# Low parts of the plain weight pages: from a VectorE subtraction to an accumulating DMA

## The chip, the cores and the metric

The kernel runs on one core of a Trainium2 chip. The core has five engines with an instruction stream each: TensorE (PE, its weight loads shown apart as PEld), VectorE (DVE), ScalarE (ACT), GpSimd (POOL) and SyncE (SP), and 16 DMA engines that serve all DMA queues. The metric is device time in microseconds (us) of one execution; lower is better.

## The reference, cut to what matters

Two layers of a decoder trunk in float32 on x of [512, 1024]. Each layer has three residual sub-layers, each ended by a layer norm: a token mixer (one wide input projection, sliding-window attention over 16 heads, a gated linear recurrence, three more 1024x1024 products), cross-attention into 256 memory tokens, and a SwiGLU block.

```python
for l in range(DEPTH):                        # DEPTH = 2
    mix = hybrid_mixer(h, w_in[l], ..., w_br_rnn[l], w_br_attn[l], sinks[l], w_out[l], cos, sin)
    h = layer_norm(DEEPNORM_ALPHA * h + mix, ln1_g[l], ln1_b[l])
    h = layer_norm(DEEPNORM_ALPHA * h + cross_attention(h, mem, cq_w[l], ckv_w[l], co_w[l]), ...)
    h = layer_norm(DEEPNORM_ALPHA * h + swiglu(h, ffn_wi[l], ffn_wo[l]), ln3_g[l], ln3_b[l])
```

All matrix products go through weights that are read once per execution from device memory.

## The kernel before, in words

**Products in three terms.** A float32 operand is held as two float32r parts, hi (the value rounded) and lo (value minus hi). A product A @ B is summed on PE from three float32r products: hi*hi, hi*lo and lo*hi (`mtile`, L259; `step` in `out_norm`, L442; the memory-value loop in `cross`, L913). The weight's hi part is used in two products of three and its lo part in the third, so of the first three matmuls of a page the third is the first to need lo.

**Weight pages.** `Weights` (L45) streams the weights as pages of [128, 1024] float32 (512 KB) in the order in which they are used; `schedule_weights` (L614) lists them, 128 plain pages per layer and 40 more that take another way (`split_quad`, the first product of the SwiGLU block, which the change does not touch). A page's life, in `split` (L94): SyncE has loaded it into one of four `raw` buffers (`dma`, L84); ACT writes the rounded copy `whi` (L110); DVE writes `wlo` = raw - whi (L111); then loads are issued until four pages past this one are under way (L113). The parts take two of the 32 pages of the pool `pg`. A raw buffer is free for the next load when both readers are done, and the SyncE queue waits for that at the load's issue; everything that SyncE issues later waits behind it.

**How far ahead.** `next` (L193) hands out page i after it has put the split of pages up to i + 2 (`la` = 2) into the instruction streams; so the split of page i + 2 stands, in the order of each engine, before the evictions of page i's product. Where a stage ends, `ensure` (L189) puts in several splits at once: the five last row pages of an output projection (L463) and some of the next stage (L466). Instructions of one engine run in the order that the framework fixed when the kernel was built, which is mostly the order of the program.

**Stages of a layer**, with their pages and PE work per page: keys, values and two query blocks (4 pages); six query and twelve gate blocks beside the attention units (18 pages, a page is 24 matmuls of 512 columns); the attention branch (8); the recurrent input with its convolution, four elementwise instructions per block on ACT and DVE (8, "conv stage" below); the recurrence's gates (4); four gate blocks with the recurrence's exponentials on ACT (4) and the GeLU gate with the scan (8), together "recurrence stage"; the recurrent branch (8); the output projection by rows (8, of which 5 are held for the end); cross-attention keys (8, 24 matmuls of only 256 columns, "key stage"); queries (8); memory values (8, 12 matmuls of 512 columns, "value stage"); the cross output projection by rows (8); the SwiGLU block's first four pages and, after the 40 others, its 22 row pages.

**GpSimd before.** It subtracts in `split_quad` (L139, 40 times), copies a sink column for each attention unit (L560, 64 times), and adds the last bias (L419). It issues no DMA.

Of the kernel before, what the change touches and what calls it, by code (L numbers as in the profile page):

```python
# [9 lines left out]
AF = mybir.ActivationFunctionType  # L10
ALU = mybir.AluOpType
AX = mybir.AxisListType
PSUM = bass.MemoryType.PSUM
# [27 lines left out]
def f(ap):  # L41
    return ap.bitcast(F32)


class Weights:  # L45
    """Streams the weights in the order in which they are used: each page of
    [128, 1024] is loaded once and split exactly into two float32r parts."""

    def __init__(self, K):
        self.K = K  # L50
# [43 lines left out]
    def split(self):  # L94
        j = self.n_split
        if j >= len(self.specs):
            return
        while self.n_dma <= j:
            self.dma()
        if j in self.quad:  # L100
            self.drain()
            self.gen = self.split_quad(j)
            self.drain()
            return
        self.n_split += 1
        nc = self.K.nc
        raw = self.raw.pop(j)
        hi = self.K.page(F32R, "whi")
        lo = self.K.page(F32R, "wlo")
        nc.scalar.activation(out=hi, in_=raw, func=AF.Copy)  # L110
        nc.vector.tensor_sub(out=lo, in0=raw, in1=f(hi))  # L111
        self.parts[j] = (hi, lo)
        while self.n_dma < min(len(self.specs), j + 1 + N_RAW):  # L113
            self.dma()

    def split_quad(self, j):
        """Operands of the seven products that replace the eight block products
        of two column blocks (rows halved, columns the two blocks)."""
        while self.n_dma <= j + 1:
            self.dma()  # L120
        self.n_split += 2
        K, nc = self.K, self.K.nc
        a, b = self.raw.pop(j), self.raw.pop(j + 1)
        a1, a2, b1, b2 = a[:, :S], a[:, S:], b[:, :S], b[:, S:]

        def one(x):
            t = K.page(F32R, "wq")
            K.split_to(t[:, :S], t[:, S:], x)
            return t[:, :S], t[:, S:]

        def pair():
            hi, lo = K.page(F32R, "wqh"), K.page(F32R, "wql")
            return [(hi[:, :S], lo[:, :S]), (hi[:, S:], lo[:, S:])]

        tt = nc.vector.tensor_tensor
        o = self.parts[j] = {}
        s12, s34 = K.page(F32, "s12"), K.page(F32, "s34")
        s1, s2, s4, s3 = s12[:, :S], s12[:, S:], s34[:, :S], s34[:, S:]
        nc.gpsimd.tensor_tensor(out=s3, in0=a1, in1=b1, op=ALU.subtract)  # L139
        tt(out=s1, in0=b1, in1=b2, op=ALU.add)  # L140
        yield
        o["A11"] = one(a1)
        yield
        tt(out=s2, in0=s1, in1=a1, op=ALU.subtract)
        o["S1"], o["S2"] = pair()
        yield
        K.split_to(*o["S1"], s1)
        yield
        tt(out=s4, in0=a2, in1=s2, op=ALU.subtract)
        yield  # L150
        K.split_to(*o["S2"], s2)
        yield
        o["A12"] = one(a2)
        yield
        o["S4"], o["S3"] = pair()
        K.split_to(*o["S4"], s4)
        yield
        K.split_to(*o["S3"], s3)
        yield
        o["A22"] = one(b2)  # L160
        while self.n_dma < min(len(self.specs), j + 2 + N_RAW):
            self.dma()
# [38 lines left out]
class Trunk:  # L201
# [66 lines left out]
    def xs(self, c0=0, c1=S):  # L268
        return lambda k: (self.xT[:, k, 0, c0:c1], self.xT[:, k, 1, c0:c1])
# [20 lines left out]
                           self.xs(hf * 256, hf * 256 + 256))  # L290
        return out

    # ---- layer norm over token tiles, and the transposed operand for what follows
    def to_xT(self, t):
        for q in range(2):
            ps = self.ps("pt")
            for i in range(4):
                c = (q * 4 + i) * P
                self.tp(ps[:, i * P:(i + 1) * P], self.xt[t][:, c:c + P])
            v = ps.rearrange("p (k s) -> p k s", k=4)  # L300
            self.split_to(self.xT[:, q * 4:q * 4 + 4, 0, t * P:(t + 1) * P],
                          self.xT[:, q * 4:q * 4 + 4, 1, t * P:(t + 1) * P], v)
            if self.want_T:
                self.x_parts(t, q, v)
        self.x_done[t] = True

    def x_parts(self, t, q, v):
        """The sums of x's blocks that the seven products take, split in two parts."""
        nc = self.nc
        tt = nc.vector.tensor_tensor  # L310
        if t < 2:
            if q == 0:
                self.Bf[t] = self.page(F32, "Bf").rearrange("p (k s) -> p k s", k=ND)
            nc.scalar.activation(out=self.Bf[t][:, q * 4:q * 4 + 4, :], in_=v, func=AF.Copy)
            return
        b = self.Bf[t - 2]
        h = lambda name: self.half(name=name).rearrange("p (k s) -> p k s", k=4)
        if q == 0:
            self.t1, self.b12 = h("t1"), h("b12")
            tt(out=self.t1, in0=v, in1=b[:, 0:4, :], op=ALU.subtract)  # L320
            nc.scalar.activation(out=self.b12, in_=v, func=AF.Copy)
            if t == 2:
                self.T = {n: [self.page(F32R, n + p).rearrange("p (k s) -> p k s", k=4) for p in "hl"]
                          for n in ("T1", "T2", "T3", "T4")}
            return
        t2, t3, t4 = h("t2"), h("t3"), h("t4")
        tt(out=t2, in0=v, in1=self.t1, op=ALU.subtract)
        tt(out=t3, in0=v, in1=self.b12, op=ALU.subtract)
        tt(out=t4, in0=b[:, 4:8, :], in1=t2, op=ALU.subtract)
        c = slice((t - 2) * P, (t - 1) * P)  # L330
        for n, x in (("T1", self.t1), ("T2", t2), ("T3", t3), ("T4", t4)):
            self.split_to(self.T[n][0][:, :, c], self.T[n][1][:, :, c], x)
        self.Bf[t - 2] = None
# [9 lines left out]
            self.tick()  # L343

    def proj_pair(self):
        """Two column blocks of x @ W; returns the first as an SBUF tile, the second
        as its halves over the tokens (one in PSUM, one in SBUF)."""
        nc = self.nc
        o = self.W.next_quad()
        b1, b2, b3 = (self.ps(n)[:, :256] for n in ("q1", "q2", "q3"))  # L350
        T = {n: (lambda k, n=n: (self.T[n][0][:, k, :], self.T[n][1][:, k, :])) for n in self.T}
        xs = lambda k0, c0: (lambda k: (self.xT[:, k0 + k, 0, c0:c0 + 256], self.xT[:, k0 + k, 1, c0:c0 + 256]))
        c1, c3 = (lambda t: (t[:, :256], t[:, 256:]))(self.half(name="c13"))
        c2, c5 = (lambda t: (t[:, :256], t[:, 256:]))(self.half(name="c25"))
        g = self.half(name="gt")
        cp = lambda out, in_: nc.scalar.activation(out=out, in_=in_, func=AF.Copy)  # L356
        add = lambda out, x, y: nc.vector.tensor_tensor(out=out, in0=x, in1=y, op=ALU.add)
        self.quad_product(b1, o["A11"], xs(0, 0), True)
        cp(c1, b1)
        self.W.piece()  # L360
        self.quad_product(b2, o["S1"], T["T1"], True)
        cp(c5, b2)
        self.W.piece()
        self.quad_product(b1, o["S2"], T["T2"], False)
        cp(c2, b1)
        self.W.piece()
        self.quad_product(b2, o["S4"], xs(4, 256), False)
        add(g[:, 256:], c2, b2)
        self.W.piece()
        self.quad_product(b1, o["S3"], T["T3"], False)  # L370
        cp(c3, b1)
        self.W.piece()
        self.quad_product(b3, o["A12"], xs(4, 0), True)
        add(g[:, :256], c1, b3)
        self.W.piece()
        self.quad_product(b1, o["A22"], T["T4"], False)
        add(c3, c3, c5)
        self.W.piece()
        return g, b1, c3
# [48 lines left out]

    def out_norm(self, act, nk, res, alpha, eps, gv, bv, last=False, prefetch=0, between=None,
                 want_T=False, restore=False):  # L430
        """x_tok <- LN(alpha * x_tok + act @ W), W streamed by rows."""
        nc = self.nc
        g = self.page(F32, "ln_g")
        nc.sync.dma_start(out=g, in_=gv.partition_broadcast(P))
# [41 lines left out]
            if between:  # L476
                between(t)

    # ---- sliding-window attention
    def rope(self, ps, eng=None):  # L480
        nc = self.nc
        sh = self.half(name="sh")
        nc.vector.stream_shuffle(sh, ps, ROPE_SWAP)
        q = self.half(name="qr")
        nc.vector.tensor_tensor(out=q, in0=ps, in1=self.ropeC, op=ALU.mult)
        eng = eng or (nc.vector if ROPE_V else nc.gpsimd)
        eng.tensor_tensor(out=sh, in0=sh, in1=self.ropeS, op=ALU.mult)
        eng.tensor_tensor(out=q, in0=q, in1=sh, op=ALU.add)
        return q
# [120 lines left out]
                                        in0=av[0:64, :, e, :], in1=t[0:64, :, e, :], op=ALU.add)  # L610
            self.split_to(ya[:, 0, cs], ya[:, 1, cs], y)

    # ---- one layer
    def schedule_weights(self):  # L614
        a, W = self.a, self.W
        for l in range(self.L):
# [453 lines left out]
```

## Time and profile before

| | us |
|---|---|
| runs shown: median of 2 (lowest, highest) | 1901.68 (1901.50, 1901.86) |
| span of the profiled execution, first to last instruction | 1899.8 |
| PE busy in it | 1881.5 (99%) |
| DVE busy | 1327.2 (70%) |
| ACT busy | 928.9 (49%) |
| POOL busy | 112.3 (6%) |
| DMA packets' share of the 16 engines' span | 37% |

The span leaves out what lies before the first and after the last instruction; the runs shown are 1.9 us longer than it. Busy time of PE contains what a pipelined matmul waits behind the one before. A row of the timeline gives the start in us from the span's start, the duration in us, engine, line, operation, the tile written and the tiles read, their shapes and types, how many instructions are merged, and in brackets the idle time of the engine just before with what ended it.

### The profile page before, as it was taken

Reading aid. Unit: us, or ns where it says so; the run is one execution under the profiler, and the core shown is the slowest. Engines: PE = TensorE matmul, PEld = TensorE weight load, DVE = VectorE, ACT = ScalarE, POOL = GpSimd, SP = SyncE. Lnnn points to the kernel's source line nnn. Section 1 sums busy time; section 2 is a strip of 40 time slices with the busy share of each in tenths; the row PEclk is TensorE's granted clock in tenths of the full one; section 3 lists DMA queues with packets and bytes.
Section 4 is the critical chain, followed back from the end, with each engine's and each line's share of the span. In section 5 each row is a group of like instructions: output and inputs, shape, how many; then the busy total and the mean of one; then the engine's idle time right before and its main releaser. Section 6 shows DMA issues by size and latency. Waiting matters only on the chain.

```text
span 1899.8 us, 27941 instructions
## 1 busy us (share of the span) xinstructions
PE 1881.5 (99%) x10874; PEld 1654.2 (87%) x10874; DVE 1327.2 (70%) x2267; ACT 928.9 (49%) x1760; POOL 112.3 (6%) x114
## 2 busy tenths in 40 slices
PE   8999999999999999999999999999999999999998
PEld 7888888889888999998898888888898889999886
DVE  5997367567557988873579963675665589888634
ACT  4676168333443665652246751773244536565521
POOL 0000000000000122100000000000000001221001
PEclk9999999999999999999999999999999999999999
DMA  6433233354244233354213441333542513333531
GB/s 171 112 101 107 60 100 89 100 177 145 67 149 129 79 112 101 109 190 139 72 45 101 110 124 45 100 89 100 177 123 78 182 63 112 100 110 102 188 100 45
DMA packets 275445, 209.19 MB, mean 110 GB/s; under 512 B 7536, under 2 KB 253808, under 8 KB 275312
## 3 DMA queue, kind: packets, MB, share of 16 engines
q1 hardware_dynamic: 275312, 207.40, 36.7%
q8 instruction: 85, 1.39, 0.3%
q14 instruction: 48, 0.39, 0.1%
HBM read 192.69 MB, written 8.39 MB: 106 GB/s over the span
## 4 chain that ended last, share of the span: by engine, by line
PE 96%; DVE 3%; DMA 1%; SPq 0%; ACT 0%; issue 0%; DVEq 0%
PE ps L232 45%; PE acc L232 21%; PE q L232 21%; PE cv L232 2%; PE sc L232 2%; PE av L232 1%; PE cs L232 1%; PE pT L236 1%; PE pt L236 1%; DMA raw<-in_w_in_dram 1%; DVE xT L253 0%; PE cT L236 0%; DVE y L405 0%; DVE st L398 0%; DVE y L396 0%; DVE nw L408 0%
## 5 line engine op out<-in xcount | busy, mean ns | idle before, releaser
L232 PE MATMUL ps<-xT,whi 128*128 128x512 f32 (+1 forms) x1984 | 563.2, 370 | 3.4 <-ACT whi L110 2.3
L111 DVE TENSOR_TENSOR wlo<-raw,whi 128x1024 fp32r<-128x1024 f32 x256 | 310.6, 1222 | 142.0 <-ACT whi L110 113.9
L232 PEld LDWEIGHTS ps<-xT,whi 128*128 128x128 f32 x1984 | 345.5, 189 | 58.7 <-ACT whi L110 2.7
L232 PE MATMUL ps<-xT,wlo 128*128 128x512 f32 (+1 forms) x992 | 363.2, 367 | 0.8 <-DVE wlo L111 0.8
L110 ACT ACTIVATE whi<-raw 128x1024 fp32r<-128x1024 f32 x256 | 266.5, 1053 | 126.9 <-PE acc L232 52.4
L232 PE MATMUL acc<-whi,hs 128*128 128x512 f32 x704 | 217.9, 390 | 0.5 <-ACT hs L252 0.5
L232 PEld LDWEIGHTS ps<-xT,wlo 128*128 128x128 f32 x992 | 187.2, 189 | 34.1 <-DVE wlo L111 1.0
L232 PEld LDWEIGHTS acc<-whi,hs 128*128 128x128 f32 x704 | 132.1, 188 | 28.3 <-ACT hs L252 0.9
L139 POOL TENSOR_TENSOR s<-raw 128x512 f32<-128x512 f32 x40 | 82.9, 2074 | 1209.6 <-DVE y L405 878.4
L232 PE MATMUL acc<-wlo,hs 128*128 128x512 f32 x352 | 137.0, 389 | 0.0
L232 PE MATMUL q<-xT,wq 128*128 128x256 f32 x960 | 126.7, 281 | 0.0
L232 PEld LDWEIGHTS q<-xT,wq 128*128 128x128 f32 x960 | 119.4, 189 | 0.0
L253 DVE TENSOR_TENSOR wql<-s,wqh 128x512 fp32r<-128x512 f32 x160 | 116.7, 757 | 0.0
L252 ACT ACTIVATE wqh<-s 128x512 fp32r<-128x512 f32 x160 | 96.1, 624 | 18.9 <-DVE s L140 9.2
L356 ACT ACTIVATE c<-q 128x256 f32<-128x256 f32 x160 | 60.7, 379 | 84.5 <-PE q L232 83.1
L253 DVE TENSOR_TENSOR wq<-raw,wq 128x512 fp32r<-128x512 f32 x120 | 82.8, 690 | 0.0
L232 PE MATMUL acc<-whi,mg 128*128 128x512 f32 x256 | 80.2, 391 | 0.0
L232 PE MATMUL acc<-whi,cO 128*128 128x512 f32 x256 | 80.2, 391 | 0.0
L232 PE MATMUL ps<-ya,whi 128*128 128x512 f32 x256 | 78.9, 389 | 0.0
L232 PE MATMUL ps<-yr,whi 128*128 128x512 f32 x256 | 78.8, 389 | 0.0
L232 PEld LDWEIGHTS acc<-wlo,hs 128*128 128x128 f32 x352 | 66.1, 188 | 13.5
L252 ACT ACTIVATE wq<-raw 128x512 fp32r<-128x512 f32 x120 | 74.5, 621 | 0.0
(218 smaller groups left out, 3718.9 us busy)
## 6 DMA issues: line engine op xcount, KB each, us to landing
raw<-in_ffn_wi_dram SPq DMA_DIRECT2D x88, 512.0 KB, 3.9
raw<-in_w_in_dram SPq DMA_DIRECT2D x84, 512.0 KB, 3.9
raw<-in_ffn_wo_dram SPq DMA_DIRECT2D x44, 512.0 KB, 3.7
raw<-in_ckv_w_dram SPq DMA_DIRECT2D x32, 512.0 KB, 4.3
raw<-in_w_br_attn_dram SPq DMA_DIRECT2D x16, 512.0 KB, 3.8
raw<-in_w_br_rnn_dram SPq DMA_DIRECT2D x16, 512.0 KB, 4.0
raw<-in_w_out_dram SPq DMA_DIRECT2D x16, 512.0 KB, 3.6
raw<-in_cq_w_dram SPq DMA_DIRECT2D x16, 512.0 KB, 5.0
```

The costliest lines, as they stand in the source:

```text
L110: nc.scalar.activation(out=hi, in_=raw, func=AF.Copy)
L111: nc.vector.tensor_sub(out=lo, in0=raw, in1=f(hi))
L139: nc.gpsimd.tensor_tensor(out=s3, in0=a1, in1=b1, op=ALU.subtract)
L232: self.nc.tensor.matmul(out, lhsT=lhsT, rhs=rhs, start=start, stop=stop, **kw)
L236: self.nc.tensor.transpose(out, in_, self.ident)
L252: nc.scalar.activation(out=hi, in_=src, func=AF.Copy)
L253: nc.vector.tensor_sub(out=lo, in0=src, in1=f(hi))
L356: cp = lambda out, in_: nc.scalar.activation(out=out, in_=in_, func=AF.Copy)
```

## The change

For a plain page, ACT first writes minus hi into the tile of the low part (the page scaled by -1, rounded to float32r), then GpSimd issues a DMA that reads the raw page and adds it onto that tile, in SBUF, and then ACT writes hi as before. The VectorE subtraction is gone. The arithmetic is the same: raw + (-hi). The rest of the diff takes out docstrings and comments and leaves every line at its number up to L110.

```diff
         raw = self.raw.pop(j)
         hi = self.K.page(F32R, "whi")
         lo = self.K.page(F32R, "wlo")
+        nc.scalar.activation(out=lo, in_=raw, func=AF.Copy, scale=-1.0)
+        nc.gpsimd.dma_start(out=f(lo), in_=raw, accum_op=ALU.add)
         nc.scalar.activation(out=hi, in_=raw, func=AF.Copy)
-        nc.vector.tensor_sub(out=lo, in0=raw, in1=f(hi))
         self.parts[j] = (hi, lo)
         while self.n_dma < min(len(self.specs), j + 1 + N_RAW):
             self.dma()
```

## Rows read from the trace of the kernel before

**Rows 1.** The page, part 1: busy us of each engine (share of the span) xinstructions.
```profile
PE 1881.5 (99%) x10874; PEld 1654.2 (87%) x10874; DVE 1327.2 (70%) x2267; ACT 928.9 (49%) x1760; POOL 112.3 (6%) x114
```
**Rows 2.** Waits of PE, whole span: waiter <- releaser: us in total, times, longest.
```profile
PE ps L232 <- ACT whi L110: 2.3, 2, 1.6
PE ps L232 <- ACT xT L252: 1.0, 4, 0.3
PE ps L232 <- DVE wlo L111: 0.8, 1, 0.8
```
**Rows 3.** The page, part 5: the split's two groups; busy us, mean ns | idle before.
```profile
L111 DVE TENSOR_TENSOR wlo<-raw,whi 128x1024 fp32r<-128x1024 f32 x256 | 310.6, 1222 | 142.0 <-ACT whi L110 113.9
...
L110 ACT ACTIVATE whi<-raw 128x1024 fp32r<-128x1024 f32 x256 | 266.5, 1053 | 126.9 <-PE acc L232 52.4
```
**Rows 4.** Timeline, conv stage: a page's split on ACT, its first lo matmul.
```profile
228.84 1.04 ACT L110 ACTIVATE whi<-raw 128x1024 fp32r<-128x1024 f32 x1
...
236.55 0.40 PE L232 MATMUL ps<-xT,wlo 128*128 128x512 f32 x1
```
**Rows 5.** DMA issues of SP: xcount, KB each, median us from issue to landing.
```profile
x_keep<-y SPq DMA_DIRECT2D x8, 512.0 KB, 2.6
...
mT<-mT_keep SPq DMA_DIRECT2D x4, 512.0 KB, 6.8
```
**Rows 6.** Timeline of SP, conv stage: one DMA's issue; start, us.
```profile
231.17 0.37 SPq L91 DMA_DIRECT2D raw<-in_w_in_dram  x1
```
**Rows 7.** Line L139, whole span: duration ns min/median/max, first and last start.
```profile
L139 POOL TENSOR_TENSOR s<-raw x40: 1281/1680/3898, 603.2 to 1747.3; 128x512 f32<-128x512 f32 x40
```
**Rows 8.** Timeline, first stage: the fourth page's split, its first lo matmul.
```profile
20.86 1.06 ACT L110 ACTIVATE whi<-raw 128x1024 fp32r<-128x1024 f32 x1 [4.93 <-DMA raw<-in_w_in_dram]
...
23.23 0.38 PE L232 MATMUL ps<-xT,wlo 128*128 128x256 f32 x1
```
**Rows 9.** Windows, recurrence stage: us, then busy us (x) of PE, PEld, DVE, ACT, POOL, PEclk, DMA share, GB/s.
```profile
280.00:304.00 24.00, 24.00 (x105) 19.49 (x104) 12.96 (x16) 23.87 (x38) 0.00 (x0) 1.00 0.38 110
304.00:316.00 12.00, 12.00 (x53) 9.63 (x53) 8.24 (x10) 11.91 (x17) 0.00 (x0) 1.00 0.15 44
```
**Rows 10.** Windows of tile whi on ACT alone, recurrence stage: us, ACT busy (x), PEclk, DMA share, GB/s.
```profile
279.00:315.00 36.00, 6.45 (x6) 1.00 0.30 88
```
**Rows 11.** Timeline, recurrence stage: the seventh of these pages on ACT, its first lo matmul.
```profile
315.10 1.05 ACT L110 ACTIVATE whi<-raw 128x1024 fp32r<-128x1024 f32 x1
...
319.93 0.40 PE L232 MATMUL ps<-xT,wlo 128*128 128x512 f32 x1
```
**Rows 12.** Timeline, key stage: two evictions, the eighth page's split, its first lo matmul.
```profile
450.71 0.38 ACT L252 ACTIVATE cK<-ps 128x256 fp32r<-128x256 f32 x1
453.60 0.38 ACT L252 ACTIVATE cK<-ps 128x256 fp32r<-128x256 f32 x1 [2.50 <-PE ps L232]
...
460.50 2.00 ACT L110 ACTIVATE whi<-raw 128x1024 fp32r<-128x1024 f32 x2
...
465.96 0.28 PE L232 MATMUL ps<-mT,wlo 128*128 128x256 f32 x1
```
**Rows 13.** Timeline, value stage: splits of its fifth to seventh page, the fifth's first lo matmul.
```profile
534.09 2.95 ACT L110 ACTIVATE whi<-raw 128x1024 fp32r<-128x1024 f32 x3
...
539.54 0.39 PE L232 MATMUL cv<-wlo,mT 128*128 128x512 f32 x1
```
**Rows 14.** Windows of the conv, key and value stages; columns as in rows 9.
```profile
444.00:468.00 24.00, 24.00 (x205) 24.00 (x203) 18.89 (x31) 12.22 (x20) 0.00 (x0) 1.00 0.54 154
530.00:550.00 20.00, 20.00 (x95) 16.54 (x94) 10.99 (x16) 9.40 (x16) 0.00 (x0) 1.00 0.64 216
228.00:280.00 52.00, 52.00 (x227) 42.20 (x226) 35.00 (x43) 28.92 (x37) 0.00 (x0) 1.00 0.30 91
```
**Rows 15.** Timeline, a split and its page's first lo matmul: attention stage, then recurrent branch.
```profile
57.12 1.05 ACT L110 ACTIVATE whi<-raw 128x1024 fp32r<-128x1024 f32 x1
...
67.27 0.39 PE L232 MATMUL ps<-xT,wlo 128*128 128x512 f32 x1
...
343.96 1.04 ACT L110 ACTIVATE whi<-raw 128x1024 fp32r<-128x1024 f32 x1
...
353.53 0.39 PE L232 MATMUL ps<-yr,wlo 128*128 128x512 f32 x1
```
**Rows 16.** Waits of SP's queue, whole span: waiter <- releaser: us in total, times, longest.
```profile
SPq L91 <- DVE wlo L111: 821.6, 207, 30.9
```

## The prediction, made before the change was run

> **What bounds the kernel now.** I read the page's busy shares first: PE is busy 1881.5 us of a span of 1899.8 [rows 1]. Then the waits of PE alone: of all that the change touches, PE waits 2.3 us for high parts and 0.8 us for a low part in the whole execution [rows 2]. So the kernel ends when PE ends, and what ACT and DVE do is hidden. Third, the split's own groups: 256 subtractions of 1222 ns on DVE and 256 copies of 1053 ns on ACT [rows 3]. Taking 310.6 us off DVE shortens nothing that PE waits for beyond those 3.1 us; no more than this can be won. The question is what the new way to a low part costs, so the view that counts is the timeline: how long before PE's first lo matmul does ACT begin the page's split? In the conv stage 236.55 - 228.84 = 7.7 us [rows 4]. I call this the lead (page and matmul are matched by counting: eight lo matmuls to a page, four in the value stage, in the order of use).
>
> **The change part by part.** Before, a low part is ready 2.3 us after the split begins (1.05 + 1.22 [rows 3]). After, it is ready at 1.05 + D, where D runs from the end of ACT's minus-hi copy over GpSimd's issue to the landing of the DMA. ACT does 256 more copies, 256 x 1.05 = 270 us in all, DVE 310.6 us less, and POOL and the DMA engines take on 256 transfers of 512 KB.
>
> No DMA of GpSimd, no accumulation and no 512 KB move within SBUF is in the trace, so D has two bounds. The shortest landing of 512 KB is 2.6 us, a plain store out of SBUF [rows 5], and SP needs 0.37 us for an issue [rows 6]: 3.0 us. The longest 512 KB row lands in 6.8 us [rows 5]; an accumulation reads two streams where a copy reads one, so twice that, and GpSimd's slowest elementwise instruction beside a busy DVE takes 3.9 us [rows 7]: 13.6 + 3.9 = 17.5 us. The value I take is the nearest row with its second stream: 2 x 2.6 = 5.2 us, plus 1.2 us for the issue (GpSimd's fastest instruction of any size is 1.28 us [rows 7], SP's issue 0.37 [rows 6]): D = 6.4 us. A page then needs a lead of 1.05 + 6.4 = 7.45 us. Below nothing it cannot go: nothing in it is removed but the subtraction, which nobody waited for.
>
> The Trainium skill, "DMA: Bandwidth & Descriptors" (Anatomy of one DMA), fits a GpSimd DMA as 2.0 us plus the bytes at 436 GB/s; 512 KB read twice gives an estimate of 2.0 + 2.4 = 4.4 us. No run here shows a DMA of that queue. Put in for D, it would give 2 x (6.9 + 2) + 3 = 21 us in the sum below, 1923 us, inside rival A.
>
> Leads under 7.45 us, stage by stage, and what each costs:
>
> - Start: the fourth page's lead is 23.23 - 20.86 = 2.4 us, ended by the load [rows 8], so nothing can be begun earlier: 7.45 - 2.4 = 5 us, once.
> - Recurrence stage: ACT is full, 23.87 us of 24 and 11.91 of 12 [rows 9]. Six pages are split in this stretch [rows 10], whose six extra copies push the seventh's split by 6 x 1.05 = 6.3 us; its lead is 319.93 - 315.10 = 4.8 us [rows 11]. The low part comes at 315.10 + 6.3 + 7.45 = 328.9, 8.9 us late. The pages behind have the same shift to catch up with but PE has moved too. 9 us per layer.
> - Key stage: a product takes 453.60 - 450.71 = 2.9 us, and each split follows an eviction; the eighth page's lead is 465.96 - 460.50 = 5.5 us [rows 12], short by 2.0. As the split moves with PE and the lead spans two products, half remains on each: 1 us on six pages. The DMA engines say as much: they are 54% busy there [rows 14], 0.54 x 2.9 = 1.6 us per page; the conv stage, 30% busy [rows 14] at 24 matmuls x 52/227 = 5.5 us a page, gives 1.7 us for a page's load, and the accumulation takes between that and twice that, so 3.3 to 5.0 us per page against 2.9. I take 7 us per layer.
> - Value stage: 12 matmuls, 2.75 us a page, engines 64% busy [rows 14], so 1.8 + 1.7 to 3.4 us per page; the fifth page's lead is 5.5 us [rows 13]. Four pages at 1.2 us: 5 us per layer.
> - Conv stage and the recurrence's gates: 7.7 against 7.45, nothing. Attention 67.27 - 57.12 = 10.1, recurrent branch 353.53 - 343.96 = 9.6 [rows 15]: nothing while D stays under 8.5. If D passes its lead, a stage pays half the excess on every page.
> - Output projections (five splits at once, ACT at 2.1 us each in place of 1.05) and the 14.8 us more of ACT in attention: 2 + 2 us per layer by estimate, since no single row prices a row of splits.
>
> Queues: the load of page j + 4 waits on SP for the readers of raw page j, today 821.6 us in 207 waits for DVE [rows 16]; it will wait for the DMA's landing, D - 1.2 = 5 us later. With four buffers this costs a load per page only where pages go by in under 3 us; it is in the key and value terms. The query halves that SP issues behind such a wait are used an attention unit later, which covers 5 us. On POOL, the sink copies queued behind a page's DMA wait for ACT's copy; they serve softmaxes whose transposes the program puts 12 us later (L573), and cost nothing. The 40 subtractions of POOL stand where no plain page is split.
>
> Sum: 2 x (9 + 7 + 5 + 4) + 5 = 55 us. The profiled execution's span is 1899.8; with the 1.9 us around it, it stands at the median, 1901.7. Forecast 1901.7 + 55 = 1957 us.
>
> **The rivals.** One us of D is worth 2 x (1 recurrence + 3 key + 2 value + 1 projections) + 1 = 15 us around 6.4.
>
> A, not slower: the landing is near the plain one and the leads cover it. Place: the key and value stages, where half the price per us lies. If both streams are read at once, D = 2.6 + 1.2 = 3.8 and a page needs 4.85, under the 5.5 of both stages; the recurrence stage pays 6.3 + 4.85 - 4.83 = 6.3 and the splits in a row 2 per layer, the start 2.5: 2 x 8.3 + 2.5 = 19, 1921 us. At the lower bound D = 3.0 the recurrence stage's 5.5 per layer and the start's 1.7 remain, 13 us: 1915. It decides at D = 5.3, where 55 - 1.1 x 15 = 38 us, 2%. For it speaks the 2.6 us row, against it the second stream and engines already at 54 to 64% [rows 14].
>
> B, slow landing: D = 10, through engines that share with the loads or a slow issue. For it: GpSimd's 1.28 us subtraction grows to 3.9 beside other work [rows 7]. The known stages pay 3.6 x 15 = 54 more; conv stage and gates pay (11.05 - 7.7)/2 = 1.7 on ten pages, recurrent branch and row pages (11.05 - 9.6)/2 = 0.7 on eleven, attention (11.05 - 10.1)/2 = 0.5 on ten: 30 per layer. 55 + 54 + 60 = 169, 2071 us. At 17.5 us every stage with a lead of two products would pay, over 2400 us. The Trainium skill, "SBUF — State Buffer" (Who interferes with whom), says that GpSimd's descriptor writing waits while DVE is in a two-port mode, and that a two-operand tensor_tensor is not such a case; no run here shows it.
>
> C, faster: DVE's relief ends PE's waits. At most 3.1 us [rows 2], 1899 us; never 2%.
>
> **How the numbers follow.** Forecast (D of 5.3 to 8.5, 1940 to 2010) 0.41; A 0.35; B 0.22; C 0.02. About 2% is what a measurement of this kernel can tell from no change. Faster is C: 0.02; within 2% is A: 0.35; slower is the forecast and B: 0.63. Range 1915, A at its lower bound, to 2090, a little beyond B's 2071; outside lie some 0.05 below and 0.12 above.
>
> **What would show it right or wrong.** Waits of PE for the DMA of wlo: about 5 us in the first stage, 9 us on one page of each recurrence stage, 1 us a page in the key and value stages, next to none in conv, attention and SwiGLU rows. Issue to landing of the new DMA near 5 us, POOL near 1 us an issue. A landing over 8.5 us, or waits spread over conv and attention pages, is B; PE waits in the first stage and the recurrence stage alone are A. The forecast is wrong in its mechanism if the time goes where PE waits for high parts, or for ACT's evictions.

## The result, and the profile after

The changed kernel takes 2023.66 us (median of 2 runs, 2021.90 to 2025.41) against 1901.68 before: ratio 1.0642, 95% interval 1.0623 to 1.0661. It is slower by 122 us. The forecast was 1957 us, slower by 55; the direction and the range held, the size did not.

The page after, parts 1 and 3 (part 3: packets, MB, share of the 16 engines' span) and rows of part 5:

```profile
span 2023.6 us, 28659 instructions
...
PE 1918.9 (95%) x10874; PEld 1670.1 (83%) x10874; DVE 1032.9 (51%) x2011; ACT 1149.3 (57%) x2008; POOL 329.2 (16%) x370
...
q0 software_dynamic: 36864, 134.23, 36.2%
q1 hardware_dynamic: 275312, 207.40, 34.1%
...
L111 POOL DMA_DIRECT2D wlo<-raw x256 | 220.4, 862 | 1147.1 <-ACT wlo L110 893.8
L110 ACT ACTIVATE wlo<-raw 128x1024 fp32r<-128x1024 f32 x256 | 269.4, 1052 | 221.9 <-DMA raw<-in_ffn_wo_dram 59.6
...
raw<-in_w_in_dram SPq DMA_DIRECT2D x84, 512.0 KB, 5.9
raw<-in_ffn_wo_dram SPq DMA_DIRECT2D x44, 512.0 KB, 5.9
```

Against [rows 1], PE has the same 10874 matmuls and two losses. It is idle 2023.6 - 1918.9 = 104.7 us where it was idle 1899.8 - 1881.5 = 18.3: 86 us more. And it is busy 37.4 us longer with the same work, in good part because its granted clock fell in places (below). Together that is the whole difference of the spans, 123.8 us. DVE is busy 294 us less, and nobody gained by it. Queue q0, which did not exist before, carries the accumulations: 36.2% of 2023.6 us over 256 of them is 2.86 us of all 16 engines for each, besides the load of its page.

Waits of PE after, whole span (us in total, times, longest), which answer to [rows 2]:

```profile
PE acc L233 <- DMA wlo<-raw: 30.1, 12, 4.2
PE ps L233 <- DMA wlo<-raw: 28.5, 21, 4.3
PE acc L233 <- ACT whi L112: 6.7, 2, 4.8
PE ps L233 <- ACT whi L112: 6.0, 4, 2.6
PE ps L233 <- DVE xT L254: 5.4, 2, 2.7
...
PE cv L233 <- DMA wlo<-raw: 4.9, 2, 2.7
PE acc L233 <- ACT hs L253: 3.7, 1, 3.7
```

A low part that has not landed makes up 30.1 + 28.5 + 4.9 = 63.5 of the 86 us; before, a late low part cost 0.8. The name of the tile that PE writes tells the stage: `acc` is a product by rows (the output projections and the SwiGLU rows), `cv` the memory values, `ps` the other plain pages. Nearly half of it is `acc`, in 12 waits; 26.0 us of these stand in the four output projections, 4.1 in the SwiGLU rows.

Stage by stage, from the first matmul on a stage's first page to the first of the next stage, read from the timelines of before and after (us, layer 0 / layer 1; the last stage of layer 1 up to its last matmul). The prediction put 2 us per layer on the output projections and 2 on attention:

| stage | before | after | loss, both layers | forecast |
|---|---|---|---|---|
| before the first weight matmul | 10.0 | 11.5 | 1.5 | 0 |
| first stage | 28.7 / 25.0 | 39.4 / 25.0 | 10.7 | 5 |
| attention, its gate blocks | 136.7 / 136.9 | 138.7 / 139.4 | 4.5 | 4 |
| attention branch, conv, recurrent branch | 132.1 / 132.1 | 132.4 / 132.3 | 0.5 | 0 |
| four gate blocks with the exponentials | 22.4 / 22.4 | 22.4 / 22.4 | 0.0 | 0 |
| recurrence's gates and GeLU gate | 66.6 / 66.6 | 75.3 / 74.9 | 17.0 | 18 |
| key stage | 24.8 / 24.8 | 29.7 / 29.4 | 9.5 | 14 |
| queries | 55.9 / 55.9 | 57.0 / 57.0 | 2.2 | 0 |
| value stage | 36.8 / 36.8 | 42.1 / 44.0 | 12.5 | 10 |
| two output projections | 92.5 / 90.6 | 113.6 / 114.5 | 45.0 | 4 |
| SwiGLU block | 347.7 / 346.0 | 360.5 / 353.3 | 20.1 | 0 |
| sum (the spans differ by 123.8) | | | 123.5 | 55 |

The largest error stands in one row. Windows after: the first output projection, the key stage, and the attention branch, which lost nothing; then two stretches inside the projection (us, busy us (x) of PE, PEld, DVE, ACT, POOL, PEclk, DMA share, GB/s):

```profile
419.00:481.00 62.00, 51.61 (x230) 41.14 (x229) 24.43 (x52) 24.75 (x35) 7.56 (x9) 0.92 0.90 229
481.00:511.00 30.00, 26.10 (x211) 25.13 (x209) 11.13 (x23) 18.99 (x27) 6.21 (x8) 1.00 0.97 215
...
190.00:233.00 43.00, 43.00 (x192) 35.63 (x191) 7.15 (x14) 18.49 (x21) 7.74 (x9) 1.00 1.00 214
...
429.00:447.00 18.00, 12.11 (x51) 8.82 (x49) 0.00 (x0) 2.39 (x3) 1.17 (x2) 0.98 1.06 299
447.00:454.00 7.00, 2.50 (x5) 1.71 (x6) 0.00 (x0) 6.02 (x7) 3.13 (x4) 0.50 1.10 220
```

The DMA engines' share is 1.00 even in the attention branch, and PE still loses nothing there: a page lasts 5.5 us on PE, and the engines' time per page is 2.86 us for the accumulation and some 1.7 us for the load (the prediction's estimate from the conv stage), together less than that. (The share adds up the packets' times and reads up to 1.10 in these rows.) Where PE wants pages faster, it waits. Timeline of the first projection, on ACT, POOL, SP and PE:

```profile
425.80 1.04 ACT L110 ACTIVATE wlo<-raw 128x1024 fp32r<-128x1024 f32 x1
...
427.73 1.06 ACT L110 ACTIVATE wlo<-raw 128x1024 fp32r<-128x1024 f32 x1
428.69 1.04 ACT L112 ACTIVATE whi<-raw 128x1024 fp32r<-128x1024 f32 x1
445.34 1.06 ACT L110 ACTIVATE wlo<-raw 128x1024 fp32r<-128x1024 f32 x1 [15.61 <-DMA raw<-in_w_out_dram]
...
423.35 0.86 POOL L111 DMA_DIRECT2D wlo<-raw  x1 [4.55 <-ACT wlo L110]
425.24 0.86 POOL L111 DMA_DIRECT2D wlo<-raw  x1 [1.03 <-ACT wlo L110]
427.14 0.86 POOL L111 DMA_DIRECT2D wlo<-raw  x1 [1.03 <-ACT wlo L110]
429.08 0.86 POOL L111 DMA_DIRECT2D wlo<-raw  x1 [1.08 <-ACT wlo L110]
...
431.51 5.20 SPq L91 DMA_DIRECT2D raw<-in_w_out_dram  x2
...
428.39 0.39 PE L233 MATMUL acc<-whi,mg 128*128 128x512 f32 x1
428.62 0.39 PE L233 MATMUL acc<-wlo,mg 128*128 128x512 f32 x1
...
440.19 0.50 PE L233 MATMUL acc<-wlo,mg 128*128 128x512 f32 x1 [2.15 <-DMA wlo<-raw]
...
444.02 0.50 PE L233 MATMUL acc<-wlo,mg 128*128 128x512 f32 x1 [2.18 <-DMA wlo<-raw]
...
447.40 0.79 PE L233 MATMUL acc<-whi,mg 128*128 128x512 f32 x1 [1.96 <-ACT whi L112]
...
452.29 0.79 PE L233 MATMUL acc<-wlo,mg 128*128 128x512 f32 x1 [4.10 <-DMA wlo<-raw]
...
455.01 0.63 PE L233 MATMUL acc<-wlo,mg 128*128 128x512 f32 x1
455.44 0.63 PE L233 MATMUL acc<-whi,mg 128*128 128x512 f32 x1
```

The last five row pages of a projection are held, and each token tile goes through all five. For the first token tile PE spends six matmuls on a page, 6 x 0.23 (428.62 - 428.39) = 1.4 us, so five low parts are wanted 1.4 us apart (in a product by rows the second matmul of a page already needs lo). The four accumulations shown, for the third to the sixth row page, are issued 1.9 us apart, as fast as ACT makes the minus-hi copies. By the trace's records of the landings they land at 431.45, 436.32, 440.14 and 443.97: 8.1, 11.1, 13.0 and 14.9 us after their issues and 3.8 to 4.9 us apart. So they queue, each with its 2.86 us of engine time and the loads beside it, and PE's waits end at 440.19 and 444.02, where the last two land. A lead of 7.45 us is no guard here: the page whose split begins at 425.80 is first used at 440.19, 14.4 us later, nearly twice what the prediction asks for, and PE still waits 2.15 us for it.

These four pages fill the four raw buffers, so the load of the seventh page goes out only at 431.51, when the accumulation of the third has landed, and ACT sits 15.61 us before it. Then PE waits for the high part (447.40) and for the low part (452.29) of that page. In this stretch the granted clock is 0.50, the 1.2 GHz level; the matmuls stand 0.43 us apart (455.01, 455.44) where they stood 0.23 apart. By the trace's clock record, stretches at 0.50 hold 54 us of PE's busy time after, 3 us before: about 25 of the 37 us of longer busy time. The other 12 were not divided.

### The profile page after: what moved, and what is told of

Read it like the earlier page. It is cut to its first block, busy times and chain, and to the rows that moved or that the text cites. A ratio compares the mean times of both kernels' runs of the same rounds, so it can differ in the third digit from the quotient of the medians.

```text
span 2023.6 us, 28659 instructions
## 1 busy us (share of the span) xinstructions
PE 1918.9 (95%) x10874; PEld 1670.1 (83%) x10874; DVE 1032.9 (51%) x2011; ACT 1149.3 (57%) x2008; POOL 329.2 (16%) x370
## 3 DMA queue, kind: packets, MB, share of 16 engines
q0 software_dynamic: 36864, 134.23, 36.2%
q8 instruction: 85, 1.39, 0.3%
## 4 chain that ended last, share of the span: by engine, by line
PE 51%; issue 27%; DMA 17%; ACT 2%; DVE 2%; POOL 1%; SPq 1%; POOLq 0%; DVEq 0%; ACTq 0%
PE q L233 18%; PE ps L233 17%; PE acc L233 12%; DMA wlo<-raw 7%; DMA raw<-in_w_in_dram 3%; DMA raw<-in_cq_w_dram 2%; DMA raw<-in_w_out_dram 2%; DMA raw<-in_co_w_dram 1%; PE sc L233 1%; PE av L233 1%; ACT wlo L110 1%; DMA raw<-in_w_br_attn_dram 1%; DMA raw<-in_ffn_wi_dram 1%; POOL wlo L111 1%; ACT whi L112 1%
## 5 line engine op out<-in xcount | busy, mean ns | idle before, releaser
L233 PE MATMUL ps<-xT,whi 128*128 128x512 f32 (+1 forms) x1984 | 572.2, 375 | 12.2 <-ACT whi L112 6.0
L233 PEld LDWEIGHTS ps<-xT,whi 128*128 128x128 f32 x1984 | 352.8, 193 | 67.8 <-ACT whi L112 7.5
L111 POOL DMA_DIRECT2D wlo<-raw x256 | 220.4, 862 | 1147.1 <-ACT wlo L110 893.8
L110 ACT ACTIVATE wlo<-raw 128x1024 fp32r<-128x1024 f32 x256 | 269.4, 1052 | 221.9 <-DMA raw<-in_ffn_wo_dram 59.6
L233 PE MATMUL ps<-xT,wlo 128*128 128x512 f32 (+1 forms) x992 | 368.8, 373 | 20.2 <-DMA wlo<-raw 20.1
L233 PEld LDWEIGHTS ps<-xT,wlo 128*128 128x128 f32 x992 | 191.4, 193 | 59.2 <-DMA wlo<-raw 26.5
L254 DVE TENSOR_TENSOR wql<-s,wqh 128x512 fp32r<-128x512 f32 x160 | 121.2, 786 | 0.0
L254 DVE TENSOR_TENSOR hs<-h,hs 128x512 fp32r<-128x512 f32 x44 | 30.0, 691 | 151.8 <-ACT hs L253 151.8
```

Of the source, the lines that this page charges most:

```text
L110: nc.scalar.activation(out=lo, in_=raw, func=AF.Copy, scale=-1.0)
L111: nc.gpsimd.dma_start(out=f(lo), in_=raw, accum_op=ALU.add)
L233: self.nc.tensor.matmul(out, lhsT=lhsT, rhs=rhs, start=start, stop=stop, **kw)
L254: nc.vector.tensor_sub(out=lo, in0=src, in1=f(hi))
```

## The experiments

All ratios are to the kernel before on the same chip, three rounds each, with their 95% intervals. Unless the diff says otherwise, each starts from the changed kernel.

**The extra copy alone.** ACT writes minus hi, but no DMA follows, and DVE subtracts as before.

```diff
         nc.scalar.activation(out=lo, in_=raw, func=AF.Copy, scale=-1.0)
-        nc.gpsimd.dma_start(out=f(lo), in_=raw, accum_op=ALU.add)
         nc.scalar.activation(out=hi, in_=raw, func=AF.Copy)
+        nc.vector.tensor_sub(out=lo, in0=raw, in1=f(hi))
```

> ScalarE's extra copy stays, GpSimd's DMA is gone, VectorE subtracts as before; the same output. Theory (what costs is the DMA: its landing, and the raw buffers and DMA engines that it holds): the copy alone makes the recurrence stage late by its 6.3 us of shift, less the 4.8 us lead that had 0.9 us of slack, so about 5 us per layer, and little elsewhere: 1910 to 1915 us. Rival (ScalarE's 270 us of copies carry most of the 122 us): 1960 us or more.

Measured 1921.09 us, 1.0101 [1.0086, 1.0116]: 19 us, some more than expected. The GeLU gate of the recurrence stage goes from 44.8 to 50.9 us in both layers, 6.1 of the 7.7 that the changed kernel loses there, with the granted clock at 0.97. So most of the loss in that stage is ACT's 1.05 us per page in a stretch where ACT was full; at most 1.6 us of it come with the DMA. And both output projections stay at their 47.2 and 45.3 us: ACT's second copy, by itself, costs nothing there.

**Row pages alone, and all others.** Row pages are the four products by rows: 46 of 128 plain pages per layer (`self.row` holds their places). The second kernel has `not in` where the first has `in`.

```diff
-        nc.scalar.activation(out=lo, in_=raw, func=AF.Copy, scale=-1.0)
-        nc.gpsimd.dma_start(out=f(lo), in_=raw, accum_op=ALU.add)
-        nc.scalar.activation(out=hi, in_=raw, func=AF.Copy)
+        if j in self.row:
+            nc.scalar.activation(out=lo, in_=raw, func=AF.Copy, scale=-1.0)
+            nc.gpsimd.dma_start(out=f(lo), in_=raw, accum_op=ALU.add)
+            nc.scalar.activation(out=hi, in_=raw, func=AF.Copy)
+        else:
+            nc.scalar.activation(out=hi, in_=raw, func=AF.Copy)
+            nc.vector.tensor_sub(out=lo, in0=raw, in1=f(hi))
```

> Minus hi and the accumulating DMA only for the 92 pages loaded by rows (both output projections, memory values, second SwiGLU product); VectorE for the other 164. Between the profiles of before and after these stages grew by 31 + 14 + 13 + 13 us over both layers. Theory (the cost lies where pages go by fast or are split in a row): 70 us stay, 1965 to 1975 us, more than half of the loss for 36% of the DMAs. Rival (every page pays alike, 122/256 us): 92 x 0.48 = 44 us, 1946 us.

> The reverse: the accumulating DMA for the 164 pages that are not loaded by rows, VectorE for the 92 row pages. Theory: what is left of the 122 us, 50 us, 1945 to 1955 us, in the first stage, the recurrence stage, the key stage and the pages before the SwiGLU block. Rival (every page pays alike): 164 x 0.48 = 78 us, 1980 us.

Measured 1968.49 us, 1.0350 [1.0335, 1.0365], and 1947.99 us, 1.0244 [1.0227, 1.0261]; both within what was expected. The losses, 67 and 46 us, add to 113 of 122. A third of the pages makes the larger half.

**The output projections alone, and all but these.** The same branch with another condition: 16 pages per layer, places 62 to 69 and 94 to 101 of a layer's 168. The second kernel has the condition negated.

```diff
+        q = j % 168
+        if 62 <= q < 70 or 94 <= q < 102:
```

> The accumulating DMA only for the sixteen row pages per layer of the two output projections (32 of 256), the subtraction elsewhere. Theory: the 45 us that these four stages lost (47.2 to 61.2, 45.3 to 62.2, 45.3 to 52.4, 45.3 to 52.3 us) come from their own pages, whose five held row pages are split in one burst: 1935 to 1950 us. Rival: the loss is handed on by the stages around, through delayed loads and held raw buffers: 1905 to 1920 us.

> The reverse: the accumulating DMA for all pages but these 32. Theory (own burst): 2024 less 45, and some us more because the key stage and the SwiGLU block's first pages come after quieter engines: 1965 to 1985 us. Rival (handed on by neighbours): 2000 us or more.

Measured 1948.96 us, 1.0251 [1.0236, 1.0266], and 1970.20 us, 1.0360 [1.0344, 1.0377]. 32 pages of 256 cost 48 us with nothing of the change around them. PE's waits in the first:

```profile
PE acc L238 <- DMA wlo<-raw: 25.8, 12, 4.2
```

That is most of the 30.1 us in 12 waits of the changed kernel. The theory of the projections' own burst holds, and that of a loss handed on by the stages around falls. That it is the DMA and not ACT's copy in the burst is shown by the copy alone, above.

**All but the held pages.** Of a projection's eight pages only the five held ones are subtracted by DVE.

```diff
+        q = j % 168
+        if not (65 <= q < 70 or 97 <= q < 102):
```

> The accumulating DMA for all pages but the five held row pages of each of the two output projections (20 pages of 256). Theory: the burst of the five is what costs, so most of the gain of the run without all eight is there: 1970 to 1995 us. Rival: it is the rate of all eight pages: 2005 us or more.

Measured 1977.63 us, 1.0402 [1.0378, 1.0426]. Leaving 20 pages to DVE gives back 46 of the 53.5 us that leaving all 32 gives back; 39 of the 46 stand in the projections themselves. Windows of this kernel, its first projection:

```profile
419.00:468.00 49.00, 47.16 (x224) 38.91 (x224) 30.29 (x57) 20.33 (x30) 3.27 (x4) 1.00 0.80 232
```

49.4 us in place of 61.2 (47.2 before), at a clock of 1.00 throughout: in this projection the stalls and the lowered clock go together with the burst. In layer 1 it takes 49.4 us too, in place of 62.2, but there two waits of 1.2 and 0.8 us and a stretch of lowered clock are left (0.97 over the projection).

**A plain copy in place of the accumulation.** The DMA writes the raw page over the tile; the low part is then the whole page, so the products are not the reference's.

```diff
-        nc.gpsimd.dma_start(out=f(lo), in_=raw, accum_op=ALU.add)
+        nc.gpsimd.dma_start(out=f(lo), in_=raw)
```

> The same instructions and waits, but GpSimd's DMA copies the raw page over the low part where it added it (so the low part is the whole page, and the products are not the reference's). Theory (the second stream that an accumulation reads is what fills the engines and queues the bursts): engine time per DMA falls from 2.9 to some 1.7 us, landing from a median of 6.4 to about 4, and the loss from 122 to 40 to 70 us. Rival (the fixed part of a GpSimd DMA, its issue and completion, is what is waited for): landing over 5.5 us and 100 us or more lost.

Measured 1944.59 us, 1.0226 [1.0211, 1.0241]. The page's DMA part and issue row:

```profile
q0 software_dynamic: 36864, 134.23, 18.3%
...
L111 POOL DMA_DIRECT2D wlo<-raw x256 | 135.4, 529 | 1143.7 <-ACT wlo L110 880.1
...
wlo<-raw POOLq DMA_DIRECT2D x256, 512.0 KB, 4.5
```

A copy takes 18.3% x 1941.2 / 256 = 1.39 us of all 16 engines, half of the accumulation's 2.86, with the same packets and bytes in the row; it lands in 4.5 us against 6.4, and its issue keeps POOL 0.53 us against 0.86. The loss falls from 122 to 43 us, as the theory expected, of which the extra copy on ACT is 19. The first projection takes 53.5 us in place of 61.2, and the second is at its 45.3 us of before.

**The DMA without anybody waiting for it.** DVE makes every low part, ACT has no extra copy, and GpSimd adds each raw page onto one of two scratch tiles that nothing reads.

```diff
-N_PAGES = 32
+N_PAGES = 30
...
-        nc.scalar.activation(out=lo, in_=raw, func=AF.Copy, scale=-1.0)
-        nc.gpsimd.dma_start(out=f(lo), in_=raw, accum_op=ALU.add)
+        nc.gpsimd.dma_start(out=self.K.scr[j % 2], in_=raw, accum_op=ALU.add)
         nc.scalar.activation(out=hi, in_=raw, func=AF.Copy)
+        nc.vector.tensor_sub(out=lo, in0=raw, in1=f(hi))
...
```

The lines left out make the two tiles and set them to zero once.

> The subtraction makes every low part as before the change, and no extra ScalarE copy is made; GpSimd also adds each raw page onto one of two scratch tiles that nothing reads (30 pages in the pool in place of 32). So the DMAs' engine time and their hold on the raw buffers are there, and no product waits for a landing. Theory (engine time and held buffers are the larger part of the loss): 1930 to 1970 us, with the loads' median landing near the 5.9 us of the changed kernel. Rival (the loss is each low part's own lateness): 1902 to 1915 us.

Measured 1922.18 us, 1.0106 [1.0089, 1.0123], between the two expectations and nearer to the rival. Its DMA rows, and what SP's loads waited for:

```profile
q0 software_dynamic: 36864, 134.23, 37.3%
...
scr<-raw POOLq DMA_DIRECT2D x256, 512.0 KB, 7.0
```

```profile
SPq L91 <- DVE wlo L112: 522.2, 122, 28.8
SPq L91 <- DMA scr<-raw: 430.7, 117, 8.8
```

The engines are as full as in the changed kernel (37.3% against 36.2%), and the loads as slow (the median landing of `raw` from `w_in` is 6.3 us against 5.9), yet only 21 us are lost. My theory, that engine time and held buffers by themselves are the larger part, was wrong. Copy alone and DMA alone give 19 + 21 = 40; the other 82 us appear only when the product itself waits for the landing. Nor is the waiting by itself enough: the plain copy is waited for too, and with half the engine time it costs 24 us beyond ACT's copies. Differences remain: here the DMA does not wait for ACT, so it starts earlier and lets go of the raw page earlier, and the pool has two pages fewer, which was not tried alone. In the changed kernel SP's loads wait for the accumulations 1238.5 us:

```profile
SPq L91 <- DMA wlo<-raw: 1238.5, 249, 30.1
```

**More raw buffers.** Six in place of four, two pages fewer in the pool.

```diff
-N_PAGES = 32
-N_RAW = 4
+N_PAGES = 30
+N_RAW = 6
```

> Six raw buffers instead of four, paid for with two of the 32 pages of the part pool (no more fits). In the profile of the change the third to sixth row page of an output projection land 4 us apart, and the next loads wait for them because all four raw buffers are held. Theory (held raw buffers are half of the output projections' loss, the 4 us per accumulation on the engines the other half): 10 to 20 us of the 122 come back, 2004 to 2014 us. Rival 1 (the hold is all): 40 us back, 1985 us. Rival 2 (the engines' time is all, or two pages fewer cost as much): 2020 us or more.

Measured 2017.55 us, 1.0604 [1.0586, 1.0623]: 6 us back, at the edge of the two intervals, and between the expectations. The first projection takes 57.8 us in place of 61.2, the second 54.7 in place of 52.4. So more buffers, at the price of two pages, take back little of what the burst costs; what six buffers with all 32 pages would do was not shown.

**More lead.** Two pages further ahead, once only while the pages of a product by rows stream, and once everywhere.

```diff
+        la, self.W.la = self.W.la, 4
         for k in range(nk - res):
...
+        self.W.la = la
         self.W.ensure(res)
```

> In the row products the splits run four pages ahead instead of two while pages stream, so that fewer fall together where the five last pages are held. Theory (the burst of splits is what makes the output projections late): those stages' loss over both layers, 31 + 14 us, halves: 2000 to 2010 us. Rival (no burst but the DMA engines' total load): within 5 us of the change's 2024 us.

Measured 2044.19 us, 1.0754 [1.0736, 1.0772]: slower, where 14 to 24 us back were expected. The projections stay as they were (61.3 and 52.1 us in layer 0, 61.2 and 52.4 in the changed kernel); the SwiGLU block's first product goes from 229.5 to 244.4 us. The wait that is new, and what ACT does then, at the start of the SwiGLU rows:

```profile
PE acc L233 <- ACT hs L253: 21.8, 2, 11.0
```

```profile
891.62 0.62 ACT L961 ACTIVATE silu<-gt 128x512 f32<-128x512 f32 x1
892.14 0.38 ACT L357 ACTIVATE c<-q 128x256 f32<-128x256 f32 x1
902.68 1.06 ACT L110 ACTIVATE wlo<-raw 128x1024 fp32r<-128x1024 f32 x1 [10.16 <-DMA raw<-in_ffn_wo_dram]
903.64 1.04 ACT L112 ACTIVATE whi<-raw 128x1024 fp32r<-128x1024 f32 x1
904.59 1.65 ACT L253 ACTIVATE hs<-h 128x512 fp32r<-128x512 f32 x3
```

The fifth split stands on ACT ahead of the operand `hs` that the first row product needs. Its load waits for a raw buffer, ACT stands 10.16 us, and PE with it. A lead in program order is bought with the same raw buffers that the DMA holds.

```diff
-        W.la = 2
+        W.la = 4
```

This is done at each of the three places that set it to 2.

> Splits run four pages ahead in every stage (la = 4 for 2), nothing else changed. Theory (latency: a low part needs 1.05 us plus 6 to 7.5 us and the lead is too short in the key, value and recurrence stages): these stages' loss of 10, 12 and 15 us over both layers mostly goes, the first stage's 11 us and part of the output projections' stay: 1970 to 1995 us. Rival (throughput: the DMA engines or ScalarE are too slow over a stage, however early the split): 2015 us or more.

Measured 1993.85 us, 1.0483 [1.0468, 1.0499]: 30 us back, at the upper end of what was expected. The recurrence's GeLU gate is at 44.8 us again, as before the change, and the key stage at 25.2 and 25.9. The SwiGLU block's first product goes the other way, from 229.5 to 238.7 us, by the same wait for `hs` (10.8 us), and the first projection keeps 59.2 us. But there PE's waits for low parts are down from 2.15 + 2.18 + 4.10 us to one of 1.3; now it waits 4.4 us for the transposed memory tokens, whose copies stand on ACT behind four splits of the key stage's pages (444.98 to 452.57), and 2.6 us for the layer norm. The second projection is back at its 45.3 us in both layers, with the value stage in front of it at 44.1 and 44.9 us (42.1 and 44.0 in the changed kernel). So a longer lead covers the queue of a burst, and moves ACT's splits in front of other work.

**Only where the lead is long.** The DMA for the 104 pages whose lead before the change was over 7.45 us by the prediction: attention and gate blocks, both branches, conv, the recurrence's gates, six of the query pages.

```diff
+        q = j % 168
+        if 4 <= q < 42 or 54 <= q < 62 or 80 <= q < 86:
```

> Accumulating DMA for 104 of the 256 pages, those whose lead was 7.5 us or more in the profile of the kernel before (attention after its first stage, attention branch, conv stage and gates, recurrent branch, most queries); VectorE for the rest. Theory (a page with the lead costs next to nothing): the 7 us that these stages grew by in the profile, 1905 to 1912 us. Rival (every page pays alike, 0.48 us): 1952 us.

Measured 1911.26 us, 1.0049 [1.0034, 1.0064]. PE waits 2.7 us for these DMAs in the whole execution. For these pages the rule of the lead holds, but this choice, the best of those tried, still loses 9 us: PE was busy 99% of the span, so there was nothing to win, and no version here beats the kernel before.

## Why the prediction was right in direction and wrong in size

- **The bound.** "The kernel ends when PE ends", and at most 3.1 us could be won: right. DVE lost 294 us of work and nothing else became faster.
- **D.** Taken as 6.4 us from the end of ACT's copy to the landing. The landing is 6.4 us after the issue (median), and the issue starts 0.29 us after ACT's copy ends (423.35 against 423.06 in the projection): 6.7. POOL was to be busy near 1 us an issue, it is 0.86. The Trainium skill, "DMA: Bandwidth & Descriptors" (Anatomy of one DMA), gave an estimate of 4.4 us for 1 MB read; the shortest of the 256 landings is 4.5, close to it; the medians are 6.4, and 6.0 with 104 pages only. The size was right where pages come one at a time; one D for all stages was not. In the conv stage the landings are 4.5 to 6.5 us, in the first projections 4.5 to 14.9. Rival B, D = 10 everywhere, is excluded by the conv stage and the recurrent branch, which lost 0.5 us or nothing; but its sign, landings over 8.5 us, and its reason, engines shared with the loads, are found in the bursts.
- **Recurrence stage, 9 us per layer.** Measured 8.5, of which 6.1 are shown by the copy alone to be six extra copies on a full ACT. The closeness is in part luck: PE waits 3.1 us for the late low part, not 8.9, and the rest is the high part ahead of it (1.0), PE at the lower clock, 1.6 us that come with the DMA and 0.8 in the gates.
- **Key and value stages, 7 and 5 us per layer.** Measured 4.8 and 6.3. Engine time per accumulation, bounded between 1.7 and 3.4 us, is 2.86.
- **Output projections, 2 us per layer: the step that failed.** It stood as "2 + 2 us per layer by estimate, since no single row prices a row of splits", for the projections and for attention, and it counted ACT alone: 2.1 us a split in place of 1.05. Measured: 22.5 us per layer in the two projections, 45 in all, shown as their own by the two kernels that divide the pages, and for the most part as the five held pages' by the third. ACT's copies, the price that was counted, cost nothing there when they are alone. What paces the burst is the accumulations behind them: issued 1.9 us apart, they land about 4 us apart, where PE wants a page each 1.4 us. The prediction gave each page its own D and did not let one transfer queue behind another. The bound on their engine time was already in the text for the key and value stages, and should have been put beside these five pages. Of the 63.5 us that PE waits for low parts 26.0 stand in the projections, where the prediction's signs name none.
- **Attention, 2 us per layer.** Measured 2.3, but not by ACT as counted: the copies alone cost 1.1 us over both layers there. The number is luck.
- **SwiGLU rows, nothing.** The prediction gave no sum for it. Measured 12.8 us in the rows (9.3 and 3.5) and 7.3 in the first product. The waits stand where splits follow one another. ACT splits three row pages in a row at 883.11, 885.00 and 887.42 us, and PE waits 2.2 us for the first rows' low part (1.9 in layer 1). Late in layer 0's rows PE waits 3.7 us for the operand `hs`, which stands on ACT behind four splits of the next layer's pages, the first of them 9.01 us late by its load. Of the first product's 7.3 us, 3.3 appear with ACT's copies alone. Part of the 20 us is handed on by the projection ahead: with the DMA in the projections alone the block loses 4.7 us, and with the projections left to DVE it still loses 9.0. The rest between them was not isolated.
- **First stage, 5 us.** Measured 10.7. The fourth page's load comes later (ACT begins its split at 25.46 us, at 20.86 in [rows 8]), beside the first accumulations, and its low part is used at 34.22 after a wait of 4.31 us: a lead of 8.8 us where 7.45 were counted. The late load alone is also in the scratch-tile kernel (25.18 us), where no product waits for a landing; that stage loses 5.3 us there.
- **Left out: the clock.** The prediction counted stalls and took PE's work as constant. PE's busy time grew 37 us, 30% of the loss, about 25 of them in stretches whose granted clock is 0.50.
- **Queues.** "A load per page only where pages go by in under 3 us": in fact SP's loads wait 1238.5 us for the landings, against 821.6 us for DVE before [rows 16], and in a projection that holds up the seventh page's load.

What stays open is how the 82 us that need a waiting product divide between the landing as such and the later release of the raw page; the kernels here change both together.

## What to carry to other kernels

A page that goes from DVE to a DMA has two prices: the lead, which the timeline gives stage by stage, and the engines' time, which must fit between one page and the next wherever pages are wanted in a burst. Look for the bursts first (a stage's last pages, held pages, the first pages of a block), and set the DMA's engine time per page, with the loads beside it, against PE's time per page there: a median landing, or the lead of one page, does not show a queue. Relieving an engine that nobody waits for pays nothing, and each stall that it brings on PE can cost more than its length through the granted clock.

## What the runs showed of the hardware that was not expected

- An accumulating DMA of 512 KB within SBUF takes 2.86 us of all 16 engines, twice a plain copy's 1.39, though both rows show the same 36864 packets and 134.23 MB; its issue on POOL takes 0.86 us against 0.53, and the median landing is 6.4 against 4.5, the shortest 4.5 against 2.8.
- Four accumulations issued 1.9 us apart beside loads landed 8.1, 11.1, 13.0 and 14.9 us after their issues.
- DMA engines at a share of 1.00 cost PE nothing in the attention branch, and a full set of accumulations that nobody waits for cost 21 us in all, while taking 20 pages in four bursts off the DMA gave back 46.
- After waits of PE of 2.15, 2.18 and 1.96 us (438 to 447 us) the granted clock reads 0.50 (447 to 454 us), the 1.2 GHz level, and the matmuls run 0.43 us apart in place of 0.23.
